# A hybrid block on one Trainium2 core: the front's channel sums and products on VectorE alone, and another order of the last two experts' w_down

## The chip, the cores and the metric

The kernel runs on one core of one Trainium2 chip. A core has a matrix engine (TensorE, PE in the profile, with PEld for its weight loads), a vector engine (VectorE, DVE), a scalar engine (ScalarE, ACT), GpSimd (POOL) and a sync engine (SyncE, SP) that here issues the DMAs of all large weights. The engines run their own instruction streams in order and wait for one another by semaphores. The metric is the time of one execution on the device, in microseconds.

## The reference

One layer on x of 256 tokens by 1024 channels, in float32. `c` (one vector) gives six channel vectors by `w_ada`; four token mixers work on slices of one input projection; their outputs are raised to 1024 channels, gated, summed and projected; then a mixture of 32 experts, the best four of each token, and a last RMSNorm.

```python
mod = silu(c) @ w_ada[l] + b_ada[l]
shift1, scale1, gate1, shift2, scale2, gate2 = jnp.split(mod, 6, axis=-1)
h = rms_norm(x, g_norm_mix[l]) * (1.0 + scale1) + shift1
z = h @ w_in[l]                          # q, k, v of the four mixers, and the merge logits
ys = jnp.stack([y_moba, y_gla, y_ret, y_swa], axis=2)
up = jnp.einsum('bsnc,ncd->bsnd', ys, w_branch[l])
gates = jax.nn.sigmoid(merge_logits.reshape(B, S, N_BRANCHES, D))
x = x + gate1 * (jnp.sum(gates * up, axis=2) @ w_out[l])
h2 = rms_norm(x, g_norm_ffn[l]) * (1.0 + scale2) + shift2
for e in range(N_EXPERTS):               # gate_up, clamped SwiGLU, down, by the combine weight
    y = y + combine[:, e:e + 1] * (act @ w_down[e] + b_down[e])
x = x + gate2 * y
return rms_norm(x, g_final)
```

## The kernel before

**Weights and slots.** All large weights stream through a ring of slots of 128 partitions x 4096 float32 (2 MB each): five slots in the front, eight from the third mixer's turn in the merge loop on (RING 5, EXTRA 3, L33 to 38). `slot` hands them out in turn, `wtile` gives halves of 1 MB, and the DMAs stand in SP's queue in the order of the program: a DMA of a tile waits until the slot's last reader is done. A slot is named in the profile by the first tile that used it there, so `wada` and `win_m` are names for several tiles.

**The front** (to about 318 us). `ada` (L234) makes one of the modulation vectors: for a half of 512 columns of one part `s_`, two tiles of four row blocks are loaded, and `run` multiplies each row block by its entry of silu(c) and sums. The first four blocks are multiplied on ACT (L249; for s_ = 2 on POOL, L247) and added on POOL (L251), the other four are folded in by DVE (L254, `acs`). One step of such a `run` is taken by `slow_step` after each quarter of a unit, so that the sums lie between other work; `ada_end` (L260) transposes and reduces. `h_block` (L388) makes the normed input as a high and a low part, `hh` and `hl`. `split` (L335) does the same to a weight tile: ACT copies it in a shorter type (`wh`, L347), DVE subtracts (`wl`, L348); each has four buffers (WP = 4) of 512 columns. PE multiplies hh by wh, hl by wh and hh by wl (`z_part`, L352).

**z units.** `z_unit` (L364) makes 256 columns of the input projection in four quarters `kh`, each with a split of 2 x 256 columns, and 48 matmuls in all. The merge loop (L778) has 16 units, four for each mixer: a z unit, its sigmoid on ACT (L801), two splits of the mixer's `w_branch` (`wb`, 256 columns each), 12 matmuls into `pu` (L809), DVE's product with the gate (`msg`, L816), and the sum over mixers (`mix`, L817), on POOL for the second and third mixer. From the last mixer's turn on `out_split` (L768) loads `w_out`, POOL multiplies it by `gate1` (L774), and `out_mm` (L762) sums into `pw`. `out_last` (L854) adds to x.

**Experts** (from about 318 us). Experts go in pairs. Each has four tiles of `w_gate_up` (`wg`) and two of `w_down` (`wd`), 2 MB each, as whole rows (L136). `gate_up_part` (L1060) makes `ea` and `eb`, DVE and ACT the SwiGLU (`el`), PE its transpose (`eat`, L1081), `down` (L1086) the product `ed`, and `scatter` (L1100) sends it back to x. For the last pair `last_down` (L1111) replaces the last two: both experts' `w_down` come by column blocks of 256, 256, 256, 128 and 128 (LAST), and each block is finished before the next: `pdl` (L1128, expert 30 in the first half of the array's columns, 31 in the second), the gate (`ol`, L1132), `pyl` (L1135), the addition to x (L1137), the sums of squares (L1138, L1139) and the final gain (`res`, L1141). After the last block come the norm's factor `rs` (L1282 to 1284), the scaling, and four output DMAs.

## Time and profile before

| | us |
|---|---|
| three runs: lowest, median, highest | 1259.78, 1263.29, 1267.72 |
| the profiled execution: its time, its span | 1264.25, 1262.5 |
| PE busy in the span | 1172.2 (93%) |
| DVE, ACT, POOL busy | 484.4, 204.8, 131.2 |
| DMA | 469.88 MB, mean 372 GB/s |

The page and the views are of the profiled execution. Busy time of an engine says how much it did, not whether it was waited for; that is read from the chain of waits, which goes back from the last instruction, and from the windows, which give each engine's busy time in a stretch. A line stands for all instructions that it issued; the same line and shape can have several tile names. A matmul of float32 operands appears as two instructions in the trace.

### The profile page before, as it was taken

How to read it: one execution, taken by the hardware profiler on the slowest of the kernel's cores; microseconds unless marked ns; L12 is line 12 of the kernel's file. 1: busy time of each engine (PE TensorE's matmuls, PEld its weight loads, DVE VectorE, ACT ScalarE, POOL GpSimd, SP SyncE). 2: the span in 40 equal slices, each digit the busy share in tenths (PEclk: the TensorE clock that was granted, in tenths of full speed). 3: DMA queues.
4: the chain of work that ended last, by engine and by line, in shares of the span. 5: the costliest groups of instructions: out<-in, count | busy, mean ns of one | idle time of the engine just before them, and what ended most of it. 6: DMA issues, size and time to landing. Idle time of an engine off the chain costs nothing.

```text
span 1262.5 us, 14878 instructions
## 1 busy us (share of the span) xinstructions
PE 1172.2 (93%) x6204; PEld 567.7 (45%) x6204; DVE 484.4 (38%) x833; ACT 204.8 (16%) x403; POOL 131.2 (10%) x171
## 2 busy tenths in 40 slices
PE   7999999989999999999999999999989998989875
PEld 4778798987333433333333333333323332332224
DVE  3797598986342312222222223222212222132123
ACT  3458355445100000000000000000000000000001
POOL 2332213740000000000000000000000000000001
PEclk9999899999999999999999999999999999999999
DMA  9975369947889999999999999999999999999994
GB/s 324 337 248 201 133 221 341 346 160 276 320 365 396 429 427 429 427 427 428 428 428 428 428 428 428 426 428 427 429 427 428 427 428 428 428 427 428 427 382 145
DMA packets 74730, 469.88 MB, mean 372 GB/s; under 512 B 6425, under 2 KB 27010, under 8 KB 50594
## 3 DMA queue, kind: packets, MB, share of 16 engines
q1 hardware_dynamic: 74034, 467.64, 90.6%
q10 hardware_dynamic: 624, 1.23, 0.3%
q8 instruction: 50, 0.82, 0.3%
q14 instruction: 22, 0.18, 0.0%
HBM read 467.81 MB, written 1.05 MB: 371 GB/s over the span
## 4 chain that ended last, share of the span: by engine, by line
PE 61%; DMA 23%; DVE 10%; issue 2%; ACT 1%; POOL 1%; ACTq 0%; SPq 0%; POOLq 0%; DVEq 0%
DMA wd<-in_w_down_dram 13%; PE ed L1094 13%; PE ea L1067 12%; PE eb L1067 12%; DMA wg<-in_w_gate_up_dram 9%; PE pz_m L361 5%; PE py L1104 4%; PE pg L1000 2%; PE pw L765 2%; PE pu L809 1%; PE pdl L1128 1%; DMA wada<-in_w_ada_dram 1%; PE eat L1081 1%; DVE el L1045 1%; DVE el L1047 1%
## 5 line engine op out<-in xcount | busy, mean ns | idle before, releaser
L1067 PE MATMUL ea<-wg,he 128*64 128x512 f32 x1024 | 284.9, 600 | 8.9 <-DMA wg<-in_w_gate_up_dram 8.7
L1067 PE MATMUL eb<-wg,he 128*64 128x512 f32 x1024 | 283.6, 593 | 0.0
L1094 PE MATMUL ed<-wd,aT 128*64 128x512 f32 x960 | 214.6, 598 | 9.5 <-DMA wd<-in_w_down_dram 8.3
L1041 DVE TENSOR_SCALAR eg<-ea 128x512 f32<-128x512 f32 x32 | 22.1, 692 | 356.6 <-PE ea L1067 352.5
L1043 ACT ACTIVATE es<-eg 128x512 f32<-128x512 f32 x32 | 20.2, 630 | 827.9 <-DVE eg L1041 827.9
L1067 PEld LDWEIGHTS eb<-wg,he 128*64 128x64 f32 x1024 | 80.2, 137 | 146.9 <-issue 146.8
L1067 PEld LDWEIGHTS ea<-wg,he 128*64 128x64 f32 x1024 | 72.9, 137 | 145.6 <-issue 119.4
L1094 PEld LDWEIGHTS ed<-wd,aT 128*64 128x64 f32 x960 | 67.4, 137 | 143.8 <-issue 126.9
L1024 POOL TENSOR_TENSOR pc<-pm,comb 128x128 f32<-128x128 f32 x64 | 23.5, 402 | 685.2 <-PE psm L1032 624.3
L361 PE MATMUL pz_m<-hh,wl_m 128*128 128x256 f32 x256 | 73.3, 286 | 5.9 <-DVE wl_m L348 5.8
L361 PE MATMUL pz_m<-hh,wh_m 128*128 128x256 f32 x256 | 73.6, 287 | 0.0
L361 PE MATMUL pz_m<-hl,wh_m 128*128 128x256 f32 x256 | 72.1, 282 | 0.0
L1106 DVE TENSOR_TENSOR x_sb<-x_sb,py 128x512 f32<-128x512 f32 x60 | 41.3, 688 | 30.3 <-PE py L1104 30.3
L361 PEld LDWEIGHTS pz_m<-hh,wl_m 128*128 128x128 f32 x256 | 49.0, 191 | 8.0 <-DVE wl_m L348 7.7
L1104 PE MATMUL py<-oa,sm 128*128 128x512 f32 x60 | 33.8, 645 | 19.4 <-DVE oa L1098 19.4
L361 PEld LDWEIGHTS pz_m<-hl,wh_m 128*128 128x128 f32 x256 | 49.1, 192 | 0.1
L361 PEld LDWEIGHTS pz_m<-hh,wh_m 128*128 128x128 f32 x256 | 49.0, 191 | 0.3
L1097 DVE TENSOR_TENSOR oa<-ed,late 64x512 f32<-64x512 f32 x15 | 10.2, 683 | 94.6 <-PE ed L1094 94.6
L1097 DVE TENSOR_TENSOR ob<-ed,late 64x512 f32<-64x512 f32 x15 | 10.2, 682 | 91.0 <-PE ed L1094 91.0
L348 DVE TENSOR_TENSOR wl_m<-win_m,wh_m 128x512 fp32r<-128x512 f32 x44 | 42.0, 971 | 7.0 <-ACT wh_m L347 6.9
L1058 PE MATMUL ea<-bgu,ident 32*64 32x512 f32 x128 | 36.5, 612 | 0.0
L1081 PEld LDWEIGHTS eat<-ident,el 128*128 128x128 f32 x128 | 17.6, 205 | 41.0 <-DVE el L1047 39.3
(450 smaller groups left out, 1567.8 us busy)
## 6 DMA issues: line engine op xcount, KB each, us to landing
wg<-in_w_gate_up_dram SPq DMA_DIRECT2D x128, 2048.0 KB, 26.7
wd<-in_w_down_dram SPq DMA_DIRECT2D x60, 2048.0 KB, 27.0
wada<-in_w_ada_dram SPq DMA_DIRECT2D x13, 1024.0 KB, 7.4
win_m<-in_w_in_dram SPq DMA_DIRECT2D x11, 1024.0 KB
win_c<-in_w_in_dram SPq DMA_DIRECT2D x8, 1024.0 KB, 8.2
wada<-in_w_ada_dram SPq DMA_DIRECT2D x12, 512.0 KB, 7.3
wl<-in_w_down_dram SPq DMA_DIRECT2D x5, 1024.0 KB, 28.8
wada<-in_w_in_dram SPq DMA_DIRECT2D x4, 1024.0 KB, 8.1
```

The costliest lines, as they stand in the source:

```text
L348: V.tensor_tensor(lk, sk, f32(wk), ALU.subtract)
L361: T.matmul(pz[:, b * 256:(b + 1) * 256], l, r, start=(kh == 0 and b == 0 and kk == 0 and i == 0), stop=last and i == 2, skip_group_check=True)
L765: T.matmul(pw[t, hf_], m_[:, kk, t * P:(t + 1) * P], w[:, 0, :], start=(k == 0 and i == 0), stop=(k == KC - 1 and i == 2))
L1000: last_i["pg"] = T.matmul(pg[:, kk * 256:(kk + 1) * 256], chan(n2[:, t, :], k), pm[:, t].rearrange("p e s -> p (e s)"), start=(i == 0), st ...
L1024: G.tensor_tensor(pc[:, t, :, var, i ^ var, :], pv_[:, :, i, :], cv[:, :, i].unsqueeze(2).to_broadcast([P, EB // 2, CAP]), ALU.mult)
L1041: V.tensor_scalar(g, pa, 7.0, None, ALU.min)
L1058: T.matmul(pp_[64 * j:64 * j + 64, :], ident[r:r + NE, r + e:r + e + 1].to_broadcast([NE, CAP]), bgu[r:r + NE, :], start=True, stop=False, ...
L1067: T.matmul(pp_[64 * j:64 * j + 64, :], he[:, k, (e % EB) * CAP:(e % EB + 1) * CAP], w[:, i * DE + j * 512:i * DE + (j + 1) * 512], start=F ...
L1081: T.transpose(pt[:, q * P:(q + 1) * P], cols, ident)
L1094: T.matmul(pd[64 * jj:64 * jj + 64, :], aT[:, k % 4, 64 * (k // 4):64 * (k // 4) + 64], w[k % 4][:, o * 512:(o + 1) * 512], start=(k == 0) ...
L1104: T.matmul(py, s_[:, hf_, t * P:(t + 1) * P], o, start=True, stop=True)
L1106: V.tensor_tensor(yv, yv, py, ALU.add)
```

## The change

1. `ada` takes half of the rows instead of half of the columns: rows of 4 KB instead of 2 KB, and four DVE instructions of 128x1024 for each half. The multiplications on ACT and POOL and the additions on POOL are gone.
2. `split` takes up to 1024 columns in one instruction of ACT and one of DVE; WP goes from 4 to 3, of twice the size. `z_unit` has two halves instead of four quarters; a unit's two row blocks of `w_branch` become one split of 512 columns, the two halves of a `w_out` row block one of 1024.
3. `hl`, and the second and third mixer's `mix`, are on DVE. POOL no longer multiplies `w_out` by `gate1`; DVE multiplies `pw` by it in `out_last` (`gx`).
4. `last_pair` replaces `last_down`. Expert 30's `w_down` comes as whole rows and is multiplied as `ed`; its first tile is loaded before expert 31's last `wg` tile. Only expert 31's comes by column blocks, of 512, 256 and 256, each handled as two halves side by side in the array's columns. `res` is on DVE.

```diff
-WP = 4
+WP = 3
-    def ada(s_, j):
+    def ada(s_, i):
+        w = load_rows(f"wada{s_}_{i}", w_ada[0, i * 512:(i + 1) * 512, s_ * D:(s_ + 1) * D], D)
...
         def run():
-            for k in range(4):
-                if s_ == 2:
-                    G.tensor_tensor(w[k], w[k], cact[:, k:k + 1].to_broadcast([P, 512]), ALU.mult)
+            for kk in range(4):
+                k = 4 * i + kk
+                if k == 0:
+                    V.tensor_scalar(acc, w[kk], cact[:, k:k + 1], None, ALU.mult)
                 else:
-                    A.activation(w[k], w[k], AF.Copy, scale=cact[:, k:k + 1])
-                if k:
-                    G.tensor_tensor(w[0], w[0], w[k], ALU.add)
+                    V.scalar_tensor_tensor(acc, w[kk], cact[:, k:k + 1], acc, ALU.mult, ALU.add)
                 yield
-            for k in range(4, KC):
-                V.scalar_tensor_tensor(acc, w[k], cact[:, k:k + 1], w[0] if k == 4 else acc, ALU.mult, ALU.add)
-                yield
...
     def z_unit(tiles, c0, name, token, sw=False):
         pz = bank("z", f"pz_{name}")
-        for kh in range(4):
-            wh, wl = split(tiles[kh // 2][:, 2 * (kh % 2):2 * (kh % 2) + 2, c0:c0 + 256], 2, 256, f"{name}_{kh}", sw)
-            z_part(pz, wh, wl, kh, token)
-            bg()
-            slow_step()
+        for i in range(2):
+            wh, wl = split(tiles[i][:, :, c0:c0 + 256], 4, 256, f"{name}_{i}", sw)
+            for j in range(2):
+                z_part(pz, wh[:, 2 * j:2 * j + 2, :], wl[:, 2 * j:2 * j + 2, :], 2 * i + j, token)
+                bg()
+                slow_step()
...
-            (G if kk else V).tensor_tensor(hl[:, k, :], hf, f32(hh[:, k, :]), ALU.subtract)
+            V.tensor_tensor(hl[:, k, :], hf, f32(hh[:, k, :]), ALU.subtract)
...
-            for w in (wo[k], wo[k + 1]):
-                for h in range(2):
-                    c = slice(h * 512, (h + 1) * 512)
-                    G.tensor_tensor(w[:, c], w[:, c], gate1[:, c], ALU.mult)
...
-                (V if bi == 3 else G).tensor_tensor(mv, mv, sg, ALU.add)
+                V.tensor_tensor(mv, mv, sg, ALU.add)
...
-        V.tensor_tensor(x_sb[:, t, cs], x_sb[:, t, cs], pw[t, g], ALU.add)
+        tm = mp.tile([P, 512], F32, tag="t2", name=f"gx{t}{g}")
+        V.tensor_tensor(tm, pw[t, g], gate1[:, cs], ALU.mult)
+        V.tensor_tensor(x_sb[:, t, cs], x_sb[:, t, cs], tm, ALU.add)
...
+    def last_pair(e, a0, he, s_):
+        gate_up_bias(e + 1)
+        for k in range(6):
+            gate_up_part(e + 1, he, k)
+        ws = fetch(*wd_src(e, 0))
+        for k in range(6, KC):
+            gate_up_part(e + 1, he, k)
+        ws = ws + fetch(*wd_src(e, 1))
+        pd = bank("z", f"ed{e}")
...
+        aT = act_t(e + 1, swiglu(*gu.pop(e + 1), e + 1, f"{e + 1}"))
+        for q, (c, n) in enumerate(LAST):
...
+            for k in range(KC):
+                for j in range(2):
+                    T.matmul(pd[64 * j:64 * j + 64, 0:n], aT[:, k % 4, 64 * (k // 4):64 * (k // 4) + 64],
+                             w[:, k, (1 - j) * n:(2 - j) * n], start=(k == 0), stop=(k == KC - 1))
```

The first place is DVE's queue around the merge loop's unit 3 of the third mixer: `wl_m_3_0` is the first split of that unit, `wl_b_3` its branch weights, `msg_2` the product that ends the unit before, `ade` and `modT` the end of a modulation vector. Before:

```order
L348 TENSOR_TENSOR wl_m_3_0_2889<-wada_11_2682,wh_m_3_0_2888 128x512
L348 TENSOR_TENSOR wl_m_3_1_2905<-wada_11_2682,wh_m_3_1_2904 128x512
L816 TENSOR_TENSOR msg_2_2854<-pu_2_2864,msg_2_2854 128x512
L268 TENSOR_REDUCE ade_2884<-pmt_2879 128x4
L348 TENSOR_TENSOR wl_m_3_2_2921<-win_m_21_2783,wh_m_3_2_2920 128x512
L269 TENSOR_TENSOR modT<-ade_2884,bT 128x4
L348 TENSOR_TENSOR wl_m_3_3_2937<-win_m_21_2783,wh_m_3_3_2936 128x512
L348 TENSOR_TENSOR wl_b_30_2955<-wb_0_2562,wh_b_30_2954 128x256
L348 TENSOR_TENSOR wl_b_31_2959<-wb_0_2562,wh_b_31_2958 128x256
L348 TENSOR_TENSOR wl_m_0_0_2995<-win_m_00_2978,wh_m_0_0_2994 128x512
L348 TENSOR_TENSOR wl_m_0_1_3011<-win_m_00_2978,wh_m_0_1_3010 128x512
L816 TENSOR_TENSOR msg_3_2952<-pu_3_2962,msg_3_2952 128x512
```

After, at the same place:

```order
L343 TENSOR_TENSOR wl_m_3_0_2597<-wada_1_1_2414,wh_m_3_0_2596 128x1024
L343 TENSOR_TENSOR wl_m_3_1_2625<-win_m_21_2499,wh_m_3_1_2624 128x1024
L809 TENSOR_TENSOR msg_2_2558<-pu_2_2564,msg_2_2558 128x512
L265 TENSOR_REDUCE ade_2584<-pmt_2579 128x4
L810 TENSOR_TENSOR mix<-mix,msg_2_2558 128x512
L266 TENSOR_TENSOR modT<-ade_2584,bT 128x4
L343 TENSOR_TENSOR wl_b_3_2655<-wb_2318,wh_b_3_2654 128x512
L265 TENSOR_REDUCE ade_2592<-pmt_2587 128x4
L266 TENSOR_TENSOR modT<-ade_2592,bT 128x4
L343 TENSOR_TENSOR wl_m_0_0_2691<-win_m_00_2674,wh_m_0_0_2690 128x1024
L343 TENSOR_TENSOR wl_m_0_1_2719<-win_m_00_2674,wh_m_0_1_2718 128x1024
L809 TENSOR_TENSOR msg_3_2652<-pu_3_2658,msg_3_2652 128x512
```

A unit's four subtractions of 512 columns are two of 1024, its two `wl_b` of 256 one of 512; both `wl_m` of the next unit stand ahead of `msg`, where one pair stood ahead and one behind; `mix` is new in this queue.

The second place is POOL's queue in the merge loop. Before, twelve of its rows (`wada_10`, `wada_00` and `win_m_01` are the sums of `ada`, `wo_0` the gate's product):

```order
L251 TENSOR_TENSOR wada_10_2251<-wada_10_2251 128x512 x3
L817 TENSOR_TENSOR mix<-mix,msg_0_2218 128x512
L251 TENSOR_TENSOR wada_00_2457<-wada_00_2457 128x512 x3
L817 TENSOR_TENSOR mix<-mix,msg_1_2327 128x512
L817 TENSOR_TENSOR mix<-mix,msg_2_2424 128x512
L251 TENSOR_TENSOR win_m_01_2565<-win_m_01_2565 128x512 x2
L817 TENSOR_TENSOR mix<-mix,msg_3_2533 128x512
L251 TENSOR_TENSOR win_m_01_2565<-win_m_01_2565 128x512
L817 TENSOR_TENSOR mix<-mix,msg_0_2648 128x512
L817 TENSOR_TENSOR mix<-mix,msg_1_2757 128x512
L774 TENSOR_TENSOR wo_0_3185<-wo_0_3185,gate_1630 128x512 x4
L817 TENSOR_TENSOR mix<-mix,msg_2_2854 128x512
```

After, all of POOL's rows between the first norm and the experts:

```order
L306 TENSOR_TENSOR rsa_175<-msa_173,mhalf 128x1
L306 TENSOR_TENSOR rsa_182<-msa_180,mhalf 128x1
L520 TENSOR_TENSOR hrsgla<-hvargla,mhalf 128x8
L520 TENSOR_TENSOR hrsret<-hvarret,mhalf 128x8
L893 TENSOR_TENSOR ssq_3134<-ssq_3134,mhalf 128x1 x2
L917 TENSOR_TENSOR n2l<-scr,n2h 128x256 x2
```

The sums, `mix` and the products of `w_out` are gone from this queue; the head norms' factors (`hrsgla`, `hrsret`) and what follows the merge stay.

The third place is the end of PE's queue: `ea` and `eb` with `wg_3` are the last tile of expert 31, `aT_7107` and `aT_7168` (before) and `aT_6715` (after) the activations of experts 30, 31 and 30. Before:

```order
L1067 MATMUL ea_7109<-wg_3_7145,he_6738 64x512 x2
L1067 MATMUL eb_7110<-wg_3_7145,he_6738 64x512 x2
L1067 MATMUL ea_7109<-wg_3_7145,he_6738 64x512 x2
L1067 MATMUL eb_7110<-wg_3_7145,he_6738 64x512 x2
L1081 MATMUL eat_7163<-ident,el_7159 128x128 x4
L1128 MATMUL pdl_7174<-res,aT_7107 64x256 x8
L1128 MATMUL pdl_7174<-wl_7172,aT_7168 64x256 x8
L1128 MATMUL pdl_7204<-wl_7172,aT_7107 64x256
L1135 MATMUL pyl_7194<-ol_7191,sm_1_7006 128x256 x2
L1128 MATMUL pdl_7204<-wl_7202,aT_7168 64x256
```

After:

```order
L1061 MATMUL ea_6717<-wg_2_6743,he_6346 64x512 x2
L1061 MATMUL eb_6718<-wg_2_6743,he_6346 64x512 x2
L1124 MATMUL ed_6767<-wd_0_6753,aT_6715 64x256 x16
L1061 MATMUL ea_6717<-wg_3_6755,he_6346 64x512 x2
L1061 MATMUL eb_6718<-wg_3_6755,he_6346 64x512 x2
L1061 MATMUL ea_6717<-wg_3_6755,he_6346 64x512 x2
L1061 MATMUL eb_6718<-wg_3_6755,he_6346 64x512 x2
L1075 MATMUL eat_6814<-ident,el_6810 128x128 x4
L1124 MATMUL ed_6767<-wd_1_6765,aT_6715 64x256 x16
L1146 MATMUL pdl_6824<-wl_6822,aT_6819 64x256 x16
L1158 MATMUL pyl_0_6843<-oa_6800,sm_1_6614 128x256
L1158 MATMUL pyl_0_6843<-ob_6801,sm_1_6614 128x256
```

The first half of expert 30's product moved ahead of expert 31's last `wg` tile, the second behind the transpose, and the column blocks of expert 31 alone follow.

## Rows read from the trace of the kernel before

**Rows 1.** Windows table by stage: window, length, busy of PE, PEld, DVE, ACT, POOL; clock, DMA share, GB/s.

```profile
56.00:97.00 41.00, 39.34 (x278) 33.06 (x277) 40.70 (x92) 23.87 (x64) 16.16 (x12) 1.00 0.74 253
97.00:141.00 44.00, 41.57 (x307) 35.27 (x305) 27.87 (x50) 25.09 (x52) 9.45 (x6) 0.88 0.66 239
141.00:295.00 154.00, 145.54 (x1136) 138.27 (x1136) 131.18 (x188) 78.98 (x146) 60.77 (x38) 0.99 0.64 237
...
318.00:380.00 62.00, 60.34 (x258) 20.23 (x259) 20.61 (x40) 6.33 (x9) 4.25 (x11) 0.97 0.82 338
...
800.00:1220.00 420.00, 385.48 (x1722) 131.19 (x1716) 96.86 (x148) 15.57 (x26) 5.80 (x16) 1.00 1.01 427
```

**Rows 2.** The sync queue's waits, 318 us to the end: total us, times, longest.

```profile
SPq L136 <- PE eb L1067: 513.6, 118, 10.9
```

**Rows 3.** Chain of waits around 240 us: start, us, what ran or was waited for.

```profile
232.42 1.44 PE pu L809 x12
233.86 5.45 PE pz_m L361 x48
...
245.46 2.38 DVE wl_b L348 x2
```

**Rows 4.** DVE groups by form, 20 to 318 us: busy us, mean ns, idle before.

```profile
L348 DVE TENSOR_TENSOR wl_m<-win_m,wh_m 128x512 fp32r<-128x512 f32 x44 | 42.0, 971 | 7.0 <-ACT wh_m L347 6.9
...
L254 DVE SCALAR_TENSOR_TENSOR acs<-wada,cact,acs 128x512 f32<-128x512 f32 x24 | 24.8, 1035 | 0.2
...
L348 DVE TENSOR_TENSOR wl_b<-wb,wh_b 128x256 fp32r<-128x256 f32 x16 | 10.8, 684 | 0.5 <-ACT wh_b L347 0.5
...
L348 DVE TENSOR_TENSOR wl_o<-wo,wh_o 128x512 fp32r<-128x512 f32 x12 | 8.1, 686 | 2.0 <-ACT wh_o L347 1.9
```

**Rows 5.** DVE timeline: start, us, line, operation, tile; both speeds.

```profile
163.86 0.75 DVE L254 SCALAR_TENSOR_TENSOR acs<-wada,cact,acs 128x512 f32<-128x512 f32 x1
...
257.40 3.46 DVE L348 TENSOR_TENSOR wl_m<-win_m,wh_m 128x512 fp32r<-128x512 f32 x2
...
267.90 0.41 DVE L348 TENSOR_TENSOR wl_b<-win_m,wh_b 128x256 fp32r<-128x256 f32 x1
...
270.19 0.68 DVE L348 TENSOR_TENSOR wl_o<-wo,wh_o 128x512 fp32r<-128x512 f32 x1
```

**Rows 6.** POOL groups by form, 20 to 318 us: busy us, mean ns, idle before.

```profile
L251 POOL TENSOR_TENSOR wada<-wada 128x512 f32<-128x512 f32 x15 | 21.9, 1461 | 41.6 <-ACT wada L249 41.0
L774 POOL TENSOR_TENSOR wo<-wo,gate 128x512 f32<-128x512 f32 x12 | 20.1, 1708 | 0.0
...
L817 POOL TENSOR_TENSOR mix<-mix,msg 128x512 f32<-128x512 f32 x8 | 13.1, 1634 | 25.8 <-DVE msg L816 19.2 <-DMA win_m<-in_w_out_dram 6.6
...
L247 POOL TENSOR_TENSOR wada<-wada,cact 128x512 f32<-128x512 f32 x8 | 9.9, 1251 | 11.5 <-DMA wada<-in_w_ada_dram 11.5
```

**Rows 7.** Windows of 2 us around PE's clock drop, columns as in the first group.

```profile
128.00:130.00 2.00, 0.33 (x2) 0.19 (x2) 2.00 (x6) 0.00 (x0) 0.00 (x0) 1.00 0.22 16
130.00:132.00 2.00, 1.89 (x5) 1.12 (x6) 0.88 (x3) 0.00 (x0) 0.00 (x0) 0.50 0.96 344
```

**Rows 8.** PE timeline at the same place: start, us, line, tile, wait before.

```profile
129.31 0.33 PE L667 MATMUL po_gla<-z_gv,glat 64*64 64x64 f32 x2 [1.59 <-DVE glat L654]
```

**Rows 9.** Chain of waits at the end of the kernel, columns as above.

```profile
1220.12 1.08 PE ea L1067 x4
...
1225.89 0.66 PE eat L1081 x4
...
1226.54 6.26 PE pdl L1128 x34
...
1234.43 3.61 PE pdl L1128 x31
...
1248.26 2.62 PE pdl L1128 x26
```

**Rows 10.** Windows of 5 us in the tail, one of them.

```profile
1230.00:1235.00 5.00, 4.48 (x26) 2.73 (x25) 0.95 (x2) 0.00 (x0) 0.00 (x0) 1.00 1.12 341
```

More of the change, by code (lines that the diff above doesn't have):

```diff
@@ L233, in hybrid_block_kernel @@
     acs = {}
[L235 to L242 removed]
+    def ada(s_, i):
+        w = load_rows(f"wada{s_}_{i}", w_ada[0, i * 512:(i + 1) * 512, s_ * D:(s_ + 1) * D], D)
+        if i == 0:
+            acs[s_] = mp.tile([P, D], F32, tag="acs", name=f"acs{s_}", bufs=1)
+        acc = acs[s_]
@@ L801, in hybrid_block_kernel @@
             A.activation(sg, pz, AF.Sigmoid)
-            wsp = [split(wb[k][:, u * 256:(u + 1) * 256].unsqueeze(1), 1, 256, f"b{n}_{u}{k}") for k in range(2)]
+            wbh, wbl = split(wb[:, :, u * 256:(u + 1) * 256], 2, 256, f"b{n}_{u}")
             pu = bank("t", f"pu{n}_{u}")
```

173 lines of the change are left out of this document (91 added, 82 removed).

## Prediction

> **What bounds the kernel now.** I read the table by stages first, to see which engine is full where [rows 1]. From 800 us to 1220 us the DMA share is 1.01 at 427 GB/s, and PE, busy 385.48 of 420 us, is not the bound. The sync queue's waits say the same from the other side: SP waits 513.6 us, in 118 waits, for PE to finish with a slot of the ring [rows 2], so the stream of expert weights is issued as soon as there is room, and it is always behind. From 318 to 380 us PE is busy 60.34 of 62 us [rows 1], at the head of the stream. The end of the kernel is therefore the start of the expert stream plus its bytes at full rate, plus a tail; what the front gains moves everything behind it one for one, and the middle is not touched by the change.
>
> In the front (until 318 us) the DMA share is 0.64 to 0.75 [rows 1], so bytes are not what it waits for. PE is busy 39.34 of 41 us, 41.57 of 44 and 145.54 of 154 in its three stages; the idle time, 1.66 + 2.43 + 8.46 = 12.55 us, is all that better supply can give back there, beside the clock. DVE is busy 40.70 of 41 us in the first and 131.18 of 154 in the third. The chain of waits shows who is late: units of one PE kind run back to back at 5.45 us for the 48 matmuls of a z unit and 1.44 us for the 12 of pu, until at 245.46 us the chain passes to DVE for 2.38 us over two wl_b [rows 3].
>
> Why is DVE late there? The grouped DVE rows hold a slow and a fast kind of the same work [rows 4]: wl_m takes 971 ns on average, while wl_o, a subtraction of the same shape, takes 686; acs 1035, wl_b 684. Single instructions show that the averages mix two speeds [rows 5]: two wl_m take 3.46 us at 257.40, one wl_o takes 0.68 us at 270.19, one wl_b of 256 columns 0.41 us, one acs 0.75 us. What runs beside the slow ones is POOL: it is busy 16.16 + 9.45 + 60.77 = 86.4 us between 56 and 295 us [rows 1], and its rows are 128x512 additions and products, of which four kinds are 21.9, 20.1, 13.1 and 9.9 us [rows 6] (the others are the same forms under other tile names). Over uncontended times the three DVE groups lose 44 x 0.285 = 12.5 us, 24 x 0.285 = 6.8 us and 16 x 0.27 = 4.3 us.
>
> **The change part by part.**
>
> *POOL's work goes away or to DVE.* DVE gets the 8 mix additions (0.69 us each by the shape of wl_o), four hl, four products gx, and ada's whole sum. For lengths that the trace lacks I take the slope of two rows: (0.68 - 0.41)/256 = 1.05 ns per column [rows 5]. A 128x1024 subtraction is then 0.68 + 0.54 = 1.22 us, an acs of 1024 columns 0.75 + 0.54 = 1.29 us. Bounds for both: the slope alone, 1.08 us, and two instructions of 512 in a row, 1.36 and 1.50 us; I take the line through the two lengths that the trace has. The 32 acs of 512 columns become 32 of 1024: +17 us of DVE work. Against it each merged pair of subtractions saves 2 x 0.68 - 1.22 = 0.14 us.
>
> *What a merge unit then asks of DVE.* Two wl_m of 1024 columns, one wl_b of 512, msg, mix: 2 x 1.22 + 3 x 0.69 = 4.5 us against PE's 5.45 + 1.44 = 6.9 us. With four acs in it, 9.7 us. Two neighbouring units, one with acs, come to 14.2 us of DVE against 13.8 us of PE: just level, with waits possible where they stand. The two DVE pieces in the section on the change show the plain unit: the next unit's two wl_m stand ahead of msg and mix, so that mix, now on DVE, isn't in front of the work that PE wants next.
>
> *What it gives.* In the merge stage PE's idle time is 8.46 us, and its waits there end with wl_m or wl_b. I take 7 of the 8.5 as regained. In the stage 56 to 97 us DVE is full without a break, and would not be without the 9.9 and part of the 21.9 us of POOL beside it: 1.5 of 1.66 us. In the stage 97 to 141 us one wait of PE, 1.59 us, ends with a mask copy of DVE's, glat [rows 8]; it comes sooner behind a freed DVE, but acs of 1.29 us stand among these copies: 0.5 of 2.43 us. Then the clock: between 128 and 130 us PE is busy 0.33 of 2 us, and from 130 us on the granted clock is 0.50, the lower of its two levels, 1.2 GHz and not 2.4 [rows 7]; over the stage it is 0.88 [rows 1], which costs 0.12 x 44 = 5.3 us, and the smaller drop in the merge stage 0.01 x 154 = 1.5 us. Whether the drops go depends on whether PE's gaps before them become small enough, which no row shows: between 0 and 6.8 I take half, 3.5 us.
>
> The Trainium skill ("TensorE: Matmul & The Clock Gate", Part 1: The HAM clock gate) says that the lower clock is the default and activity releases it, so it would be all or nothing here: 6.8 or 0 us. The two rows at 1.00 and 0.50 in [rows 7] agree with two levels.
>
> *What it costs in the front.* Each z unit now waits for a split of 1024 columns where it began after one of 512. ACT's copy and DVE's subtraction each come about 0.5 us later. While the next unit's first split is made during the last 4 us of the running one, that is hidden; where acs stand ahead it is not. Bounds are 0 and 1.0 us for each of the 32 halves of merge units; I take 2 us in all, the units with acs, since the plain one has 2.4 us to spare. The gate product moves from 16 POOL instructions to four DVE ones behind pw. Only the last stands on the way to the end: 0.7 us.
>
> Front: 7 + 1.5 + 0.5 + 3.5 - 2 - 0.7 = **9.8 us**.
>
> *The tail.* Before, PE starts on expert 31's last wg tile at 1220.12, eat follows 5.77 us later, and all of both experts' w_down comes in column blocks after it: 34 matmuls in 6.26 us, ol and pyl in the 1.63 us to the next block, blocks of 31 and 26 in 3.61 and 2.62 us; the last ends at 1250.88, 11.6 us before the span's end [rows 9]. In that time the DMA moves 341 GB/s at share 1.12 [rows 10]: runs of 1 KB and less are slower than the stream's 16 KB. In the new order, which the two PE pieces show, the four MB of expert 30's w_down come as whole rows. By 4.9 us for a 2 MB tile at 427 GB/s: wd_0 lands about where the last wg tile did, 1220.1; the last wg tile at 1225.0, wd_1 at 1229.9, the first block of 512 columns, 2 MB in runs of 2 KB, between 1234.8 and 1236.0. PE: the first half of ed (32 matmuls of 256 columns, 3.7 us as the block of the same size) is done while it waits for the last wg tile; eat follows 5.77 us after it landed, as before, at 1230.8; the second half of ed (behind eat's 0.66) to 1235.2; pdl0 to 1238.9; two ol and twice as many pyl, between 1.63 us and twice that, by the middle 2.4, to 1241.3; pdl1 of 128 columns 2.3 us; pdl2 with the other pyl to 1246.8. Behind it 11.6 us as before and about 1.0 more, since the last block is 256 columns wide and not 128: 1259.4, a gain of **3.1 us**. Bounds: 7 us if pyl and ol are hidden by other blocks, -2 us if the last blocks land late at 341 GB/s or slower.
>
> Sum: 1264.25 (the profiled execution's own time: its span of 1262.5 and 1.75 around it) - 9.8 - 3.1 = 1251.35, **1251 us**. That execution lies 1 us over the median of the runs, 1263.29.
>
> **The rivals.**
>
> *The front runs at PE's own pace.* All 12.55 us of idle time and the 6.8 us of clock are regained, and nothing is lost but the 0.7: 18.7 us; with the tail 1264.25 - 18.7 - 3.1 = **1242 us**. For it speaks that the plain unit asks 4.5 of 6.9 us of DVE; against it the units with acs. The Trainium skill ("SBUF — State Buffer", Who interferes with whom) says that a VectorE instruction with two SBUF inputs and a GpSimd one that reads SBUF share one port, and the second to start is blocked for the other's whole time; by that rule all of DVE's excess goes with POOL's work, and this is the case that follows. The two speeds of one form in [rows 5] agree with it.
>
> *The longer serial work eats the front's gain.* The freed DVE time goes to 17 us of acs, and half units start later by as much as PE had waited before: the front gives 0 to 3 us, the tail its 3: **1259 us**. For it speaks the level sum of 14.2 against 13.8 us.
>
> *DVE becomes the bound, and the kernel is slower.* Each z half exposed costs 1.0 us. Gains of 9.8 + 2 + 3.1 = 14.9 us are used up by 15 exposed halves of the 32 in the merge loop; with 27 the kernel is 1% slower, with all 32 it takes 1264.25 - 14.9 + 32 = **1281 us**. It would show as wl_m of 1024 columns ending PE's waits in every unit. Against it speaks that three buffers of 1024 columns hold a whole unit's splits, where four of 512 held two thirds.
>
> *The change does not reach the end, because the stream is the bound from its first tile.* Then the front gives nothing. Against it: the front's DMA share of 0.64 to 0.75 leaves room to have its bytes sooner. The time would be 1261; I count it with the third case.
>
> **How the numbers follow.** Chances: forecast (1245 to 1257) 0.48; PE's pace 0.20; gain eaten 0.22; slower 0.10. One per cent, about what a measurement of this kernel can tell, is 12.6 us: faster means below 1250.7, slower above 1275.9. Faster holds a little under half of the forecast, 0.23, nearly all of PE's pace, 0.20, and 0.01 of the third case, together 0.44; slower by over 1% is 0.07 of the 0.10; the rest, 0.49, is within 1%. The range from 1239 to 1262 leaves out the slower case and the far ends of the others.
>
> **What the profile after would show.** DVE's wl_m, acs and wl_b at one speed each (1.22, 1.29 and 0.68 us), POOL nearly empty until 318 us; PE idle in the merge stage under 3 us, or else ended by wl_m; no stretch at 0.50 after the gla stage; out_last's adds about 10 us sooner; the expert stream unchanged at 427 GB/s; the last pdl 12.6 us before the end. The prediction is wrong if POOL was not what slowed DVE, if DVE's instructions of 1024 columns cost two of 512, or if acs in DVE's order hold back wl_m in more than a few units.

## The result, and the profile after

The changed kernel takes 1247.35 us (median; lowest 1245.21, highest 1248.94) against 1262.19 for the kernel before in the same rounds: ratio 0.9875, 95% interval 0.9839 to 0.9912. It is 1.25% faster, 15 us, a little under the forecast of 1251 and inside the range. The profiled execution took 1248.94 us with a span of 1247.2.

How far the lead has come at a given point is read from two places. The first matmul of expert 0 on weights (`ea` from `wg`) marks the end of the front. In the timeline of TensorE (start, us, line, operation, tile), before and then after:

```profile
319.69 1.08 PE L1067 MATMUL ea<-wg,he 128*64 128x512 f32 x4
```

```profile
303.04 1.08 PE L1061 MATMUL ea<-wg,he 128*64 128x512 f32 x4
```

The front is done 16.65 us sooner. The second place is the transpose of expert 30's activations, which starts at 1206.19 us before and at 1191.15 after: 15.04 us sooner. From there to the span's end it is 56.3 us before and 56.05 after. So the front gave more than the whole gain, and the tail gave 0.3 us. The sum of the profiled executions closes with it: 1264.25 - 16.65 + 1.6 - 0.3 = 1248.9.

The windows by stage, which answer [rows 1]:

```profile
56.00:97.00 41.00, 41.00 (x284) 34.05 (x282) 33.54 (x82) 24.83 (x60) 0.00 (x0) 1.00 0.67 249
97.00:141.00 44.00, 43.47 (x355) 37.50 (x353) 32.26 (x51) 18.99 (x30) 0.21 (x1) 1.00 0.67 240
141.00:295.00 154.00, 150.85 (x1177) 143.08 (x1175) 116.50 (x166) 65.95 (x92) 5.11 (x4) 1.00 0.72 274
...
318.00:380.00 62.00, 61.87 (x240) 19.30 (x238) 20.46 (x33) 1.54 (x3) 5.87 (x16) 0.92 0.81 335
...
800.00:1200.00 400.00, 368.10 (x1634) 125.68 (x1632) 94.02 (x144) 14.96 (x25) 5.81 (x16) 1.00 1.01 428
```

PE's idle time in the three stages is 0, 0.53 and 3.15 us, where it was 1.66, 2.43 and 8.46; the granted clock is 1.00 in all three, where it was 0.88 in the second and 0.99 in the third. But the third window is not the same work in both kernels: the changed one is some 18 us ahead by then and already in the routing from 285.82 us on, where its first transposes of the last norm (`pnt`) start. In the kernel before they start at 304.01 us. Cut there, the stage before and after, and behind it the changed kernel's routing up to the first `ea`:

```profile
141.00:304.01 163.01, 154.55 (x1176) 145.71 (x1176) 138.65 (x202) 83.56 (x154) 60.77 (x38) 0.99 0.66 246
141.00:285.82 144.82, 143.90 (x1114) 138.22 (x1112) 110.08 (x146) 60.58 (x78) 3.99 (x2) 1.00 0.74 281
285.82:303.04 17.22, 14.12 (x104) 10.01 (x102) 12.46 (x38) 8.46 (x20) 2.53 (x4) 0.90 0.52 178
```

For the same work PE is idle 8.46 us before and 0.92 after. The lead is 18.2 us at `pnt`; the routing, 15.68 us long before and 17.22 now, takes 1.5 of them back. In it the clock is at 0.50 for 3.4 us, from 294.8 us on, where the kernel before has 1.00.

POOL's 86.4 us up to 295 us are down to 5.3. And although DVE took over POOL's additions, it is busy less in the third window: 116.50 us of 154 instead of 131.18. Why is seen in the groups of DVE (141 to 295 us; busy, mean ns, idle before), which answer [rows 4, 5]:

```profile
L343 DVE TENSOR_TENSOR wl_m<-win_m,wh_m 128x1024 fp32r<-128x1024 f32 x21 | 25.7, 1226 | 13.1 <-ACT wh_m L342 13.1
L247 DVE SCALAR_TENSOR_TENSOR acs<-wada,cact,acs 128x1024 f32<-128x1024 f32 x11 | 14.2, 1287 | 0.0
L810 DVE TENSOR_TENSOR mix<-mix,msg 128x512 f32<-128x512 f32 x12 | 8.3, 688 | 0.0
...
L343 DVE TENSOR_TENSOR wl_b<-wb,wh_b 128x512 fp32r<-128x512 f32 x7 | 4.8, 686 | 0.0
```

Each form has one speed now: 1.226 us for 1024 columns (all `wl_m` lie between 1.215 and 1.242), where two of 512 took 1.94 on average and 3.46 in the slow case. What DVE now waits for in front of `wl_m` is ACT's copy. The longest waits of PE in the same stretch (total us, times, longest) say that a split holds PE back once; those of `pl` belong to the routing:

```profile
PE pl L868 <- DVE x1T L866: 1.6, 2, 0.9
PE pz_m L356 <- DVE wl_m L343: 0.7, 1, 0.7
```

Before, these were all waits in that stretch:

```profile
PE pz_m L361 <- DVE wl_m L348: 5.8, 6, 1.7
PE pu L809 <- DVE wl_b L348: 2.5, 4, 1.0
```

The stream behind is what it was: its share is 1.01 at 428 GB/s, and the sync queue waits for PE as before, which answers [rows 2]:

```profile
SPq L136 <- PE eb L1061: 509.2, 117, 10.9
```

The tail did not go as forecast. The chain of waits there, which answers [rows 9]:

```profile
1209.85 1.08 PE ea L1061 x4
...
1215.71 0.63 PE eat L1075 x4
1216.34 5.29 PE ed L1124 x32
1221.63 3.48 PE pdl L1146 x32
...
1229.08 1.14 DVE res L1166
...
1230.25 0.30 DVE oa L1151
```

The 32 matmuls of 256 columns that make the second half of `ed` take 5.29 us, and the 32 of the same size behind them 3.48. Windows of 2 us there tell them apart by the clock (columns as in [rows 7]):

```profile
1213.00:1215.00 2.00, 0.51 (x4) 0.00 (x0) 1.80 (x4) 0.63 (x1) 0.00 (x0) 1.00 1.02 373
...
1217.00:1219.00 2.00, 2.00 (x12) 1.12 (x10) 0.07 (x1) 0.00 (x0) 0.00 (x0) 0.50 0.97 337
```

PE is busy 0.51 of 2 us while DVE and ACT make expert 31's SwiGLU, and then the clock is at its lower level, 1.2 GHz, as after the gap in [rows 7].

### The profile page after: what moved, and what is told of

Its sections match the earlier page's. It is cut to its first block, busy times and chain, and to the rows that moved or that the text cites. A ratio compares the mean times of both kernels' runs of the same rounds, so it can differ in the third digit from the quotient of the medians.

```text
span 1247.2 us, 14486 instructions
## 1 busy us (share of the span) xinstructions
PE 1167.0 (94%) x6208; PEld 563.5 (45%) x6208; DVE 453.7 (36%) x769; ACT 177.1 (14%) x293; POOL 37.5 (3%) x107
## 4 chain that ended last, share of the span: by engine, by line
PE 69%; DMA 23%; DVE 6%; ACT 1%; issue 1%; POOL 0%; ACTq 0%; SPq 0%; POOLq 0%
DMA wd<-in_w_down_dram 16%; PE ea L1061 13%; PE eb L1061 13%; PE ed L1088 12%; PE pz_m L356 7%; DMA wg<-in_w_gate_up_dram 5%; PE py L1098 4%; PE pg L994 2%; PE pw L760 2%; PE pu L802 2%; PE eat L1075 1%; DVE el L1039 1%; DVE el L1041 1%; PE psm L1026 1%; DVE es L1040 1%
## 5 line engine op out<-in xcount | busy, mean ns | idle before, releaser
L1091 DVE TENSOR_TENSOR oa<-ed,late 64x512 f32<-64x512 f32 x15 | 10.2, 683 | 94.6 <-PE ed L1088 94.6
L1091 DVE TENSOR_TENSOR ob<-ed,late 64x512 f32<-64x512 f32 x15 | 10.2, 683 | 90.9 <-PE ed L1088 90.9
L1075 PE MATMUL eat<-ident,el 128*128 128x128 f32 x128 | 23.8, 308 | 13.0 <-DVE el L1041 12.9
```

Source lines behind the costliest of these rows:

```text
L1075: T.transpose(pt[:, q * P:(q + 1) * P], cols, ident)
```

## The experiments

My theory after the result was: the gain is the front's, it comes because DVE no longer shares anything with POOL's reads, and the tail gives nothing because of the lower clock and of DVE's order in it. The rivals: the larger instructions of DVE and ACT do it (fewer, longer splits), or ada's new form alone does it; for the tail, that bytes landing late set its end. Medians are given beside those of the kernel before, run beside it on the same chip; ratios are worked out by rounds and so are not quite the quotient of the medians.

**Front and tail apart.** First the new front with the old `last_down`:

```diff
-LAST = ((0, 256), (512, 128), (768, 128))
+LAST = (256, 256, 256, 128, 128)
...
-                res = last_pair(e, a0, he, sm[r])
-                break
...
+            if e + 2 == NE:
+                res = last_down(e, (a0, a1), sm[r])
+                break
```

> The new front with the old tail (both experts' w_down by column blocks, the old last_down). If the gain is the front's alone, as the two traces' first matmul of the experts (319.76 and 303.11 us) suggests: the time of the changed kernel, 1247, within 2 us, and from expert 31's first matmul behind eat to the end the same 56 us as before. If the tail gave its predicted 3.1 us: 1250 to 1251.

It took 1247.96 us against 1261.69, ratio 0.9898 (0.9877 to 0.992), and the front ended at 302.54. Then the old front with the new `last_pair`:

```diff
-WP = 3
+WP = 4
...
-    def ada(s_, i):
+    def ada(s_, j):
...
-    def split(src, nk, ncol, name, sw=False):
+    def split(src, nk, ncol, name, sw=False, pool=None):
```

> The old front with the new tail. If the tail gives nothing, the time before, 1262, within 2 us; if it gives the predicted 3.1 us, 1259. PE's clock shows which: if it falls to the lower level behind the gap before eat as it does in the changed kernel, the second half of ed takes 5.3 us and the tail gives about 0.3; if it stays, 3.7 us and about 1.9.

It took 1262.53 us, ratio 1.0009 (0.9991 to 1.0028). The whole gain is the front's; the new order at the end gives nothing that can be measured. The chain of this kernel shows the same slow block at the same place:

```profile
1232.74 0.63 PE eat L1081 x4
1233.37 5.29 PE ed L1128 x32
1238.66 3.48 PE pdl L1150 x32
```

**Is it POOL's reads?** To the changed kernel, POOL gets back 48 subtractions of 128x512, four in each unit of the second to fourth mixer, on a `msg` tile that is no longer needed. Nothing that counts waits for them:

```diff
+            for i in range(4 if bi else 0):
+                G.tensor_tensor(sg, sg, sg, ALU.subtract)
```

> The changed kernel, and in each merge unit of the second to the fourth mixer POOL subtracts the unit's dead msg tile from itself four times (48 instructions of 128x512, about 60 to 75 us of POOL, as much as POOL had in the merge stage before); nobody waits for them but the tile's next use two units later. If DVE was slow because POOL reads SBUF beside it: wl_m rises from 1.22 us to over 1.6 us on average in that stretch, PE's idle time in the merge stage rises from 3 us to 6 us or more, and the time by 4 to 9 us, to 1251 to 1256. If the gain came from fewer and longer instructions or from a relieved ACT: wl_m stays at 1.22 us and the time at 1247, within 1.5 us.

It took 1261.04 us against 1261.69, ratio 0.9998 (0.9983 to 1.0013): the whole gain is gone. The front ends at 314.88, 11.8 us later than in the changed kernel. Its groups of POOL and of DVE from 141 to 295 us:

```profile
L812 POOL TENSOR_TENSOR msg<-msg 128x512 f32<-128x512 f32 x48 | 76.0, 1583 | 60.7 <-DVE mix L810 56.6 <-DVE modT L266 1.2
```

```profile
L343 DVE TENSOR_TENSOR wl_m<-win_m,wh_m 128x1024 fp32r<-128x1024 f32 x21 | 29.8, 1425 | 8.4 <-ACT wh_m L342 8.3
...
L343 DVE TENSOR_TENSOR wl_o<-wo,wh_o 128x1024 fp32r<-128x1024 f32 x6 | 9.3, 1542 | 3.2 <-ACT wh_o L342 3.2
L809 DVE TENSOR_TENSOR msg<-pu,msg 128x512 f32<-128x512 f32 x12 | 8.2, 680 | 0.0
```

and PE's waits there:

```profile
PE pz_m L356 <- DVE wl_m L343: 6.2, 4, 2.3
```

`wl_m` goes from 1.226 to 1.425 us, `wl_o` to 1.542, and PE is idle 9.24 us from 141 us to the first `pnt` (297.26 us), where it was 0.92. `msg`, whose one input lies in PSUM, stays at 0.68. My expected length for `wl_m` was too high and the expected time too low: the loss on DVE was smaller than I thought and cost more. The counter-test keeps POOL as busy, but with writes: 120 fills of 128x512 and 12 small subtractions.

```diff
+            if bi:
+                G.tensor_tensor(sg[:, 0:8], sg[:, 0:8], sg[:, 0:8], ALU.subtract)
+            for i in range(10 if bi else 0):
+                G.memset(sg, 0.0)
```

> As the run with POOL's 48 idle subtractions, but POOL writes zeros into the dead msg tile (ten memsets of 128x512 in a unit, behind one subtraction of 8 columns that holds them at their place), so that it is as busy and reads nothing from SBUF. If it is POOL's reads that slow DVE: wl_m stays at 1.22 us and the time at 1247, within 1.5 us. If any work of POOL does, a shared write path included: wl_m over 1.4 us and 1255 to 1262, as with the subtractions.

It took 1250.3 us, ratio 0.9918 (0.9896 to 0.9941). In its profile POOL is busy 76.51 us of the stage, and neither DVE nor PE shows it: PE is busy 150.85 us as in the changed kernel, and the front ends at 303.56. The median is 2 us above the range that I expected; the profiled execution is its fastest, 1247.42. The unedited changed kernel took 1252.31 us on another chip (below), so 3 us of time prove nothing here, and the trace does.

```profile
L814 POOL MEMSET msg<- 128x512 f32 x120 | 63.7, 531 | 6.9
```

```profile
L343 DVE TENSOR_TENSOR wl_m<-win_m,wh_m 128x1024 fp32r<-128x1024 f32 x21 | 25.5, 1220 | 13.1 <-ACT wh_m L342 13.1
```

So it is not that POOL works, but that it reads: its reads cost DVE's instructions with two inputs in SBUF their speed, its writes nothing. The Trainium skill ("SBUF — State Buffer", Who interferes with whom) states this difference, and that an instruction with at most one SBUF input is spared outside VectorE's two-port modes; `wl_m` at 1.425 us beside reads and 1.220 beside writes and `msg` at 0.680 agree.

That it was so in the kernel before as well can be read there instruction by instruction. Of its 64 `wl_m` of 512 columns between 56 and 300 us, 39 have no POOL instruction beside them, and none of these takes over 0.694 us; all 17 slow ones, 1.09 to 1.775 us long, overlap one.

**Is it the size of the splits?** The units' splits of 1024 columns are made as two instructions of 512 each on ACT and DVE, everything else as changed:

```diff
+        elif nk == 4:
+            for j in range(2):
+                h = slice(2 * j, 2 * j + 2)
+                A.activation(wh[:, h], src[:, h], AF.Copy)
+                V.tensor_tensor(wl[:, h], src[:, h], f32(wh[:, h]), ALU.subtract)
```

> The changed kernel, with each split of 1024 columns in a z unit issued as two instructions of 512 on ACT and on DVE, into the same buffers and in the same order. If the longer instructions hold PE back, as the prediction's term of 2 us has it: 1 to 2 us faster, 1245 to 1246. If their fewer fixed costs are what made room: DVE's busy time up by 32 x 0.14 = 4.5 us in the merge stage, PE's idle time up, and 2 to 5 us slower. If neither matters: 1247, within 1 us.

It took 1251.37 us, ratio 0.9909 (0.988 to 0.9939). In the merge stage PE is busy 150.15 us against 150.85 and DVE 118.48 against 116.50. The front ends 3.9 us later, but only 0.7 of them are there at `pnt` (286.56 us): in this execution the clock was low for 10.2 us from 299 us on, and in the changed kernel's for 3.4 us, which is 3.4 us of work apart. By the time alone, 4 us over the result's, the expectation that the fewer fixed costs made room would fit; but DVE's busy time rose by 2.0 us and not by 4.5, and PE lost 0.7. The size is worth some 0.7 us, in neither direction the reason.

**Which of POOL's work was it?** From both ends. The kernel before with nothing changed but `ada`:

```diff
-    def ada(s_, j):
+    def ada(s_, i):
+        w = load_rows(f"wada{s_}_{i}", w_ada[0, i * 512:(i + 1) * 512, s_ * D:(s_ + 1) * D], D)
...
-                    A.activation(w[k], w[k], AF.Copy, scale=cact[:, k:k + 1])
-                if k:
-                    G.tensor_tensor(w[0], w[0], w[k], ALU.add)
+                    V.scalar_tensor_tensor(acc, w[kk], cact[:, k:k + 1], acc, ALU.mult, ALU.add)
```

> The kernel before with the new ada alone (by rows, on DVE only); mix, hl, the gate's product and the splits of 512 columns stay. POOL is rid of about 46 of its 86 us, which by the same loss gives DVE 13 us back, and DVE gets 17 us of work. If only DVE's sum counts: within 3 us of the time before, 1258 to 1263, with acs still slowed beside mix and the gate's products. If ada's sums as a chain over ACT, POOL and DVE were what held the old front, as the run with that chain in the new kernel suggests by its 1274 us: 1250 to 1254.

It took 1256.24 us against 1262.58, ratio 0.9951 (0.9933 to 0.997), between the two expectations. The front ends at 309.75, 9.9 us sooner than before. Its windows show which stages it mends:

```profile
56.00:97.00 41.00, 41.00 (x292) 34.85 (x291) 34.23 (x89) 25.80 (x69) 0.00 (x0) 1.00 0.70 255
97.00:141.00 44.00, 43.63 (x359) 37.37 (x357) 32.32 (x62) 20.91 (x43) 0.00 (x0) 1.00 0.65 240
141.00:295.00 154.00, 146.73 (x1126) 138.66 (x1124) 134.08 (x193) 72.78 (x135) 43.81 (x26) 1.00 0.69 262
```

Up to 141 us PE is as busy as in the whole change; from there POOL's 43.81 us of `mix` and gate products keep DVE at 134.08 us and PE idle for 7.27. The clock is 1.00 in all three, so the 6.8 us that it cost before are back with `ada` alone. The other end is the changed kernel with `mix` and the gate products on POOL again, without `gx`:

```diff
+            for w in (wo[k], wo[k + 1]):
...
+                    G.tensor_tensor(w[:, c], w[:, c], gate1[:, c], ALU.mult)
...
-                V.tensor_tensor(mv, mv, sg, ALU.add)
+                (V if bi == 3 else G).tensor_tensor(mv, mv, sg, ALU.add)
...
-        V.tensor_tensor(tm, pw[t, g], gate1[:, cs], ALU.mult)
```

> The changed kernel, with mix of the second and third mixer and the products of w_out and gate1 on POOL again (24 instructions of 128x512, about 39 us of POOL). By the loss of the run with idle subtractions (DVE lost 21 us to 76 us of POOL), DVE loses about 11 us here and is rid of 5.5: PE's idle time in the merge stage rises from 3 to 5 to 7 us, and the time by 3 to 6 us, to 1250 to 1253. If ada's sums on POOL were the whole of the old front's loss: 1247, within 1.5 us.

It took 1251.74 us, ratio 0.9914 (0.9892 to 0.9935). By the traces the front ends at 307.02: 4.0 us of the 16.65 are lost again. At `pnt` (290.75 us) it is 4.9 us, of which 2.9 are PE's idle time, 3.81 us where it was 0.92, and 1.7 a stretch of 3.4 us at the lower clock from 222.9 us on; without `gx` the routing then gives 1 us back. I had expected 5 to 7 us of idle time, so the forecast time came out with a smaller loss than it was built on. And the time doesn't show the loss: the unedited changed kernel took 1252.31 us on the same chip (below). PE waits for `wl_m` 2.7 us, in two waits, and POOL's own additions are the slowest of this size in all runs:

```profile
L814 POOL TENSOR_TENSOR mix<-mix,msg 128x512 f32<-128x512 f32 x8 | 16.3, 2035 | 51.4 <-DVE msg L813 51.4
```

At `pnt` the kernel with `ada` alone is 9.9 us ahead of the kernel before, and this one 4.9 us behind the changed kernel: 14.8 of the 18.2 us of lead there. The rest is smaller parts or what the two do only together.

Then the reverse of `ada`'s change on the changed kernel: its first four row blocks are scaled on ACT and added on POOL, as one instruction of 1024 columns each.

```diff
-                if k == 0:
-                    V.tensor_scalar(acc, w[kk], cact[:, k:k + 1], None, ALU.mult)
+                if i == 0:
+                    A.activation(acc if k == 0 else w[kk], w[kk], AF.Copy, scale=cact[:, k:k + 1])
+                    if k:
+                        G.tensor_tensor(acc, acc, w[kk], ALU.add)
```

> The changed kernel, with the first four row blocks of each ada sum multiplied on ACT again and added on POOL (12 additions of 128x1024, by twice the 1.25 us of 512 columns some 30 us of POOL); DVE is rid of 16 instructions, about 20 us. If what counts is the time that DVE loses beside POOL's reads, the loss can be taken from the run before: there 76 us of POOL cost DVE about 21 us, so 30 to 40 us cost 8 to 11 and 20 are freed; the merge stage is as full or a little better, 1245 to 1250. If it was ada's sums on POOL, as a chain that others wait for, that held the old front: 1255 or more, with PE's waits ended by acs or modT.

The first expectation failed by much: 1273.76 us, ratio 1.0112 (1.0078 to 1.0146), slower than the kernel before and past the second one's 1255. POOL is busy only some 33 us from 56 to 295 us. Single instructions of the timeline at 213 us show what a long POOL instruction does to the DVE instructions beside it:

```profile
213.11 0.15 DVE L268 TENSOR_TENSOR modT<-ade,bT 128x4 f32<-128x4 f32 x1
...
214.06 7.39 POOL L247 TENSOR_TENSOR acs<-acs,wada 128x1024 f32<-128x1024 f32 x3 [27.91 <-ACT acs L245]
...
214.50 1.98 DVE L268 TENSOR_TENSOR modT<-ade,bT 128x4 f32<-128x4 f32 x1
...
216.72 2.52 DVE L741 TENSOR_TENSOR wr<-wr_sb,G 128x256 f32<-128x256 f32 x1
...
219.16 3.38 DVE L345 TENSOR_TENSOR wl_m<-wb,wh_m 128x1024 fp32r<-128x1024 f32 x1
```

The three additions take 2.4 us each, one right behind the other. An instruction of four columns, 0.15 us when alone, takes 1.98 us beside the first: it lasts until that one is over. One of eight columns (`G`, 0.17 us) starts just ahead of the next addition and is spared; `wr` and `wl_m` fare like the first with the second and the third: POOL's three end at 221.45, and `wl_m` ends at 222.54, about its own length later. `modT` and `wr` are short (`wr` takes 0.42 us in the changed kernel), and each is delayed by most of an addition. What PE waits for in this kernel from 56 to 318 us:

```profile
PE pz_m L358 <- DVE wl_m L345: 9.1, 4, 3.7
PE po_gla L664 <- DVE glat L651: 4.5, 2, 3.4
```

Four waits make 9.1 us: it is not the mean of `wl_m` (1.222 us over 21) that costs, for only the one above is itself held. The longest wait, 3.69 us until 187.9, ends with a `wl_m` of 1.21 us that stands in DVE's order behind `modT` (2.12 us), `yh` (2.32) and `yl` (2.72), held one after the other by three additions from 178.78 to 186.15. `yh` is a cast with one SBUF input, 0.43 us in the changed kernel: that form is not spared. DVE also waits 4.4 us once, in its own order, for POOL's sum before it can fold in the second half; the 3.4 us for `glat` stand right behind that. ACT has the scaling again. By 295 us PE has been idle 12.1 us more than in the changed kernel, and the granted clock was 0.92 from 97 to 141 us and 0.98 to 295 (3.5 + 3.1 us). Of the 8.2 us by which the front ends behind that of the kernel before (327.85 and 319.69), 3.6 are there at `pnt`, and 4.6 come in the routing, where the clock was at 0.50 for 10.2 us. Why the first part is slower than the kernel before, where POOL did the same sums in twice as many instructions half as long, I can only argue from the length of the blocks; no run has both sizes.

**The tail.** Three edits: three filler matmuls on the SwiGLU's tiles while PE waits for `eat`; the second half of `ed` behind `eat`, its k from 4 on; `res` of a block behind the next block's `oa`, the last one behind `rs`.

```diff
+        if e == NE - 1:
+            wm = bank("t", "warm")
+            for v in (g, g, sg):
+                T.matmul(wm, ident, v, start=True, stop=True)
...
+        for k in range(4):
...
+        aT = act_t(e + 1, swiglu(*gu.pop(e + 1), e + 1, f"{e + 1}"))
+        for k in range(4, KC):
...
+            if behind:
+                with tc.issue_after(o_i):
+                    behind.pop()()
```

> The changed kernel with two edits in the tail: three matmuls on SwiGLU's intermediate tiles, whose result nobody reads, fill PE's gap before eat, and DVE makes each block's final gain behind the next block's gate and the last one behind rs. If the clock's fall before the second half of ed is what took the tail's gain: that half takes 3.7 instead of 5.3 us; the edits on DVE take 0.3 to 0.4 us from each later block and about 0.6 from the end; from eat to the end about 2.9 us less than 31.5, a total near 1244.5. If the clock falls all the same: about 1.3 us less.

The chain of this kernel at its end:

```profile
1213.76 2.78 PE warm L1044 x6
1216.54 0.44 PE eat L1079 x4
1216.97 3.60 PE ed L1135 x32
1220.58 4.12 PE pdl L1157 x42
...
1229.71 1.47 PE pdl L1157 x22
1231.18 0.02 issue
1231.20 0.30 DVE oa L1162
```

The granted clock stays at 1.00 from 1213 to 1221 us, `ed` takes 3.6 us, `oa` follows the last `pdl` at once, and from `eat` to the span's end it is 26.9 us instead of 31.5. From the landing of expert 30's first `w_down` tile (1205.3 us) to the end it is 38.1 us, where the changed kernel takes 42.15 and I had predicted 39.3. In time: 1246.11 us against 1260.56, ratio 0.9884 (0.9861 to 0.9906), 1.2 us under the changed kernel's median in the result. The third rival, bytes that land late, shows in neither chain: behind expert 31's last `wg` tile (1209.8 us in the changed kernel) no piece of it is a DMA. Since 1.2 us are within what executions differ by, the kernel ran once more, beside the changed kernel on one chip. First the changed kernel, without an edit:

> The changed kernel once more, unedited, for the comparison with the next run on the same chip: 1246 to 1249.

and the kernel with the three edits above:

> The run with both edits in the tail once more, against the changed kernel on the same chip. The trace of the first one took 38.1 us from the landing of expert 30's first w_down tile to the end, the changed kernel 42.15: if these 4 us are real, the median is 3 to 4.5 us under that of the run before this, 1243 to 1245; if they are within what executions differ by, less than 2 us under it.

1252.31 us (1245.97 to 1254.69) for the changed kernel and 1249.89 (1244.11 to 1252.05) with the three edits, against 1262.58; ratios 0.9898 (0.9875 to 0.992) and 0.9899 (0.988 to 0.9918). The chain shows the tail's 4 us again (`ed` in 3.6 us, 27.3 us from `eat` to the end), the time does not: the medians are 2.4 us apart, between what I expected if the 4 us are real and if not, and the two intervals lie on one another. For the change itself this second measurement gives 1.0% instead of 1.25%.

**What varies then?** The profiled execution of the changed kernel on that chip was a long one, span 1253.0. Its window behind the front, and its first `ea`:

```profile
295.00:318.00 23.00, 21.69 (x88) 11.58 (x89) 9.77 (x36) 6.22 (x13) 1.97 (x3) 0.63 0.48 164
```

```profile
309.23 1.98 PE L1061 MATMUL ea<-wg,he 128*64 128x512 f32 x4
```

The same program ends its front 6.2 us later than in the first profile, where the clock in this window was 0.93; here it is 0.63, and the four `ea` take 1.98 us and not 1.08. Of the 6.2 us, 1.85 are there at `pnt` (287.67 us), and were there at the first `po_gla` (127.05 us and 125.22); the other 4.3 come in the routing. In every profiled execution with the new front the lower clock starts 7 to 14 us behind the first `pnt`, behind single transposes and small matmuls, and lasts between 3.4 and 17.1 us; the kernel before, the one with the old front and the new tail, and the one with `ada` alone have no such stretch there. What in the new front brings it is open. A second such place is in the first profile around 353 us:

```profile
352.00:356.00 4.00, 4.00 (x8) 1.07 (x8) 3.43 (x5) 0.00 (x0) 0.00 (x0) 0.60 1.00 426
356.00:360.00 4.00, 3.99 (x9) 0.77 (x7) 0.69 (x1) 0.00 (x0) 2.70 (x8) 0.50 0.45 193
```

There 10.2 us at 0.50 stand where the kernel before had 3.4 in the same stage; this is where most of the 1.6 us went that the lead lost between 303 and 1191 us: it is 16.4 us at the transposes (`eat`) of experts 0 and 1 (324.89 and 339.05 us), 15.0 at those of expert 2 (385.95), and stays near that. In the second run with the tail's edits, with 3.4 us at 0.50 in that place, it is 16.5 on both sides of it. I tried to hold the clock at the first place with two filler matmuls between the last norm's transposes and the router's:

```diff
+        if g == 1:
+            fm = bank("t", f"fm{t}")
+            T.matmul(fm, ident, gate1[:, 0:512], start=True, stop=True)
```

> The changed kernel with two matmuls of 512 columns, whose result nobody reads, in PE's gaps between the last pnt and pl at the end of the front. If the gaps there bring the clock down (0.50 from 294.9 to 298.3 us in the changed kernel, longer in the two runs of the first set that have its front): no fall there, the first expert matmul 1.7 us sooner or more, 1244 to 1246. If it falls all the same, no change within 0.5 us, or 0.5 us later, since the fillers lie ahead of pl.

It did not help, and neither expectation held: 1250.71 us, ratio 0.9909 (0.9883 to 0.9934). The clock fell at 300.0 us instead, for 10.2 us, and the front ended at 306.13. What decides the length of such a stretch is open.

## Why the prediction was right, and where its terms were off

The direction, the cause and the size of the whole were right: 1251 forecast, 1247.35 measured. Not all terms were, and how near the total came is partly luck.

- *DVE's speeds.* `wl_m` 1.22, acs 1.29, `wl_b` 0.68 were forecast from a line through two lengths; measured 1.226, 1.287 and 0.686. That one instruction of 1024 columns costs less than two of 512 holds.
- *PE's idle time.* 7 of 8.46 forecast for the merge stage, 7.5 measured up to the first `pnt` (the window up to 295 us, with 5.3, holds part of the changed kernel's routing); 1.5 of 1.66 and 0.5 of 2.43 in the stages before, measured 1.66 and 1.90. Together 9.0 forecast, 11.1 measured. The second stage was under-sized: I held the acs between the `glat` copies against it [rows 8], and they cost nothing that PE saw.
- *The clock.* I took half of 6.8 us for want of a row. All of it came: no stretch before 294 us is at 0.50. This is the front's term that was most off, by 3.3 us. The sign that I gave for it, no stretch at 0.50 after the gla stage, did not hold further on: the one from 294.8 us on is new. The reading that it is all or nothing, put in the prediction beside the rule of the Trainium skill ("TensorE: Matmul & The Clock Gate", Part 1: The HAM clock gate), fits this stage.
- *The longer splits.* 2 us of loss forecast; PE waits for `wl_m` once, 0.7 us, and halving the splits moved PE's busy time by 0.7 us. With three buffers of 1024 columns, the splits stay ahead of PE.
- *`gx`.* 0.7 us forecast. The two last groups of transposes (`pnt`) start 2.23 us apart in the changed kernel and 0.95 in the one without `gx`: about 1.3 us.
- *Front in all.* 9.8 forecast, 16.65 measured: 18.2 at `pnt`, less 1.5 in the routing. Idle time (11.1) and clock (6.8) make 17.9 of the 18.2; what is left is the difference of two smaller things, a PE that is busy 1.3 us less in the first 56 us and needs 1.6 us less for the work up to `pnt`. The routing's 1.5 have two sources in sight: `gx`, and the new stretch at the lower clock, in which the 16 `pb` matmuls take 3.30 us instead of 2.03. The forecast had no term for the second.
- *The tail.* 3.1 us forecast, 0.3 measured. From the first `w_down` tile's landing to the end I had 39.3 us, and it took 42.15. The step that failed is "the second half of ed (behind eat's 0.66) to 1235.2", 3.7 us: it took 5.29, for PE stood almost idle ahead of it and its clock had fallen. I had the clock in the front's sum and did not look for the same thing at the end, though the new order puts PE's longest dense block right behind its longest wait there. The last `pdl` then ends 13.4 us before the end where 12.6 was forecast: `res` now stands on DVE ahead of the next block's `oa`, 1.22 us for 1024 columns ahead of the second block's and 0.69 for 512 ahead of the last's. With both mended the tail takes 38.1 us. So the sum of bytes and matmuls was right, and the place of the waits was not.

Of the rivals, "the front runs at PE's own pace" describes the front better than the forecast does: its 18.7 us are 16.65 in the trace, and 18.2 at `pnt`. The forecast's 9.8 lay 8.9 below it: 3.6 of idle time, 3.3 of clock and 2 for the splits. The runs give 2.1 and 3.3 of the first two to the rival, and of the 2 us for splits a wait of 0.7 is left. The total lies between the rival's 1242 and the forecast because of the routing and of the tail. "The gain is eaten" and "DVE becomes the bound" fell with DVE's 116.50 us of 154, and "the stream is the bound" with the first `ea` at 303.04 and 15 us of it still there at 1191.

The errors, too little in the front and too much in the tail, partly cancelled: 6.85 us under-sized there, 2.8 us over-sized here, and 1.6 us lost between. That they leave only 2.4 us in the profiled execution is luck.

## What to carry to other kernels

Where DVE is nearly full, elementwise work on POOL that reads SBUF is not free help: 48 idle subtractions took back a gain of 15 us, and as much POOL time in writes took nothing from the front; so take such work off POOL, even onto DVE, and look for forms with two speeds in the trace. When a change makes PE wait ahead of a dense block, price the block at the lower clock too, and count behind it what DVE has queued ahead of the next block's first operand. Sum idle time and clock by stage, each from its own window, cut the windows of two kernels where the same work ends and not at the same time, and give a term that has no row its two ends rather than a half.
